# The down product of a Strassen-style MLP: another first half product, weights loaded at other steps, the last sums at another place

## The chip, the cores and the metric

The kernel runs on one NeuronCore of one Trainium2 chip. The metric is the device time of one execution, in microseconds (us). The kernel before takes 2855.52 us, the median of 3 runs (2850.24 to 2856.83). The engines are called by their names: TensorE (PE in the profile: matmuls; PEld its weight loads), VectorE (DVE), ScalarE (ACT), GpSimd (POOL) and SyncE (SP), which only issues transfers here. GpSimd issues transfers too, in order with its other work.

## The reference, cut to what matters

The program is one step of a two-layer encoder trunk for 1072 tokens (16 meta, 32 sample, 1024 prompt), width 1024. Each layer has a mixer and then an MLP, all in 32-bit floating point:

```python
def mlp(h, w_up, w_down):
    u = jax.nn.relu(h @ w_up)
    return (u * u) @ w_down
...
xp = xp + mlp(rmsnorm(xp, norm_mlp[l]), w_up[l], w_down[l])
xs = xs + mlp(rmsnorm(xs, norm_mlp[l]), w_up[l], w_down[l])
```

`w_up` is 1024 x 4096 and `w_down` 4096 x 1024. The change touches only the second product, `(u * u) @ w_down`, in both layers.

## The kernel before, in words

Every full-precision product is made of three matmuls of a high and a low part (`mm3`, lines 72 to 77): high by high, high by low, low by high. `hi_lo` (lines 62 to 68) makes the parts: ScalarE casts the high part (line 64), and VectorE (line 66) or GpSimd (line 68) subtracts it from the source to get the low part. The profile therefore shows nearly all such work under lines 64, 66 and 68, and the tiles tell what it is: `md_w` is a weight of the down product, `md_u` a pair of rows of its activations.

The MLP is done as seven half-size products in place of eight (Strassen's scheme in Winograd's form). **Up** runs over 16 blocks of 256 hidden units. For each, TensorE makes seven products; VectorE squares the results and subtracts them from each other, so that seven operands of the down product (B11, B21, B22, T1 to T4) lie in `xT`, and GpSimd's queue stores them to a buffer `ud` in memory, 1.9 MB per block (lines 987 to 1006). The store of the last block is kept back, and line 1088 issues it in the down product.

**Down** runs the seven products of `DOWN` (line 1010), each for two column halves c, so 14 half products, written (n, c) here. One has 16 steps kb. A step is 12 matmuls (four output blocks of three) with the weight `md_w{kb}` and one row of the activations; `acts` loads two rows at a time from `ud` into one of three buffers `md_ur` and splits them into one of four buffers `md_u`. During the half c = 1 of product n, `weights(n + 1, kb)` makes the weights of the next product as TensorE is done with the old ones (line 1122). The operands of the weights are quarters of `w_down`: A11, A12, A21, A22. Two are kept in `k1` and `k2`, four tiles of 1 MB each; the others come as `md_raw`, 256 KB each, in one of three buffers. A11 and A22 and A12 need no sums. S2 needs two on VectorE for each kb (A21 + A22, less A11: lines 1036 and 1037), S3 one (line 1041) and a copy on ScalarE, A22 one behind it (line 1055), S4 one (line 1047).

In the order before, A11 is the first product. Its quarter is loaded into `k1` in four transfers on SyncE's queue at the start, and A21 into `k2` in four on GpSimd's queue at steps 2, 6, 10 and 14 of (0,0). The low halves of the first three weights and of the first activations are made on GpSimd. S2 is the second product, so that its sums are made in (0,1).

The results are added to `xT` (line 1134), which holds the residual again: it was saved to memory (`xsave`) and is loaded back at step 4 of the products 0 to 3 (line 1116). A load on GpSimd's queue stands behind a copy of one element (`behind`, line 1068) that reads the current `md_u` and writes into the load's target; the load so waits for the cast of that pair.

What sets the order: TensorE runs in the order of the code. SyncE and GpSimd run in the order of the code up to (1,0), where `order.close()` stands; after that, and VectorE and ScalarE always, a scheduler sets the order by its own estimate of times when the program is built. Each engine then works through its queue in order.

Of the kernel before, what the change touches and what calls it, by code (L numbers as in the profile page):

```python
# [51 lines left out]
class Core:  # L52
# [879 lines left out]
    def up(self, sb, ps):  # L932
# [20 lines left out]
        for at, (b, n) in enumerate(todo):  # L953
# [39 lines left out]
            elif wn == "S3":  # L993
                squared(v["B22"], v["B22"])
            elif wn == "A22":
                tt(v["B21"], v["B21"], v["B21"], op=ALU.mult)
            elif wn == "S4":
                squared(v["B12"], v["B12"])
                for x, p, m in (("T1", "B12", "B11"), ("T2", "B22", "T1"), ("T3", "B22", "B12"), ("T4", "B21", "T2")):
                    tt(v[x], v[p], v[m], op=ALU.subtract)  # L1000
                store = partial(nc.gpsimd.dma_start, self.ud[b // 4][:, b % 4], place[:, b % 2, 1:8, :hw])
                if b < self.NP - 1:
                    store()
                else:
                    self.last_store = store
                del pairs[b]
# [3 lines left out]
    DOWN = (("A11", "B11", ("11",)), ("S2", "T2", ("12",)), ("S3", "T3", ("22",)), ("A22", "T4", ("21",)),  # L1010
            ("A12", "B21", ("11",)), ("S1", "T1", ("22", "12")), ("S4", "B22", ("12",)))


    def down(self, k1, k2, sb, ps, mid, done):
# [15 lines left out]
        def weights(n, kb, eng="v"):  # L1030
            x = self.DOWN[n][0]
            a, b = (k[kb // 4][:, kb % 4] for k in (k1, k2))
            if x == "A11":
                src = a
            elif x == "S2":
# [22 lines left out]
        def acts(n, c, g):  # L1058
# [4 lines left out]
            self.hi_lo(t, hl[:, 0], hl[:, 1], "g" if (n, c) == (0, 0) and g < 2 else "v")  # L1063
# [24 lines left out]
        self.last_store()  # L1088
        at = 0
        out = {}  # L1090
        for n, c in passes:
            x, _, to = self.DOWN[n]
            first = n in (0, 4, 5, 6)
# [4 lines left out]
            for kb in range(NP):  # L1098
# [18 lines left out]
                for ob in range(4):  # L1117
                    f = slice(P * ob, P * ob + P)
                    hl = w[n, kb]
                    self.mm3(out[c][ob], (hl[:, 0, f], hl[:, 1, f]), (u[:, 0, kb % 2], u[:, 1, kb % 2]), first and kb == 0, kb == NP - 1, n in (1, 2, 3))  # L1120
# [17 lines left out]
    def mlp(self, nms, mid, done):  # L1138
# [7 lines left out]
        with ExitStack() as st, tc.manual_schedule(engines={mybir.EngineType.PE}):  # L1146
# [14 lines left out]
            k2, k1 = ([kp.tile([P, 4, 512], F32, name=f"md_k{x}{y}") for y in range(4)] for x in (2, 1))  # L1161
# [679 lines left out]
```

## Time and profile before

| | before |
|---|---|
| median of 3 runs | 2855.52 us (2850.24 to 2856.83) |
| the profiled execution | 2860.78 us, span 2859.0 us |
| TensorE busy | 2642.7 us (92%) |
| VectorE busy | 1891.1 us (66%) |
| ScalarE busy | 1265.2 us (44%) |
| GpSimd busy | 631.0 us (22%) |
| down product of layer 0 | about 977 to 1328 us |
| down product of layer 1 | about 2490 to 2857 us |

Times in a row are microseconds from the start of the span. A row of the order of time gives the start, the duration, the engine, the line, the operation, out<-in with shapes and the count, and in brackets how long the engine sat idle before it and which engine's work ended that. A row by stretches gives the stretch, its length, each engine's busy time with its number of instructions (PE, PEld, DVE, ACT, POOL), the granted TensorE clock, the busy share of the transfer engines and GB/s. Matmuls are pipelined: how fast TensorE goes is read from the distance of the starts.

### The profile page before, as it was taken

The page shows a single profiled execution, that of the slowest core. Times are in us where ns is not written, and L with a number is a line of the kernel's source. Part 1 is how long each engine was busy: PE and PEld are TensorE (multiplying, and loading weights), DVE is VectorE, ACT ScalarE, POOL GpSimd, SP SyncE. Part 2 cuts the span into 40 slices and gives each one's busy share as a digit, 9 for nine tenths or more (in the row PEclk, how much of TensorE's full clock was granted, in tenths as well). Part 3 has the DMA queues.
Part 4 walks back from the last instruction along what each step waited for, and adds up shares of the span by engine and source line. Part 5 has one row for each costly group of instructions (what it writes and reads, how often), then busy time and mean ns, then how long its engine had stood idle before and what let it go on. Part 6 is the DMA issues. An engine that isn't in the chain of part 4 may idle for free. (4 is left out here: it accounts for less than half of the span.)

```text
span 2859.0 us, 49166 instructions
## 1 busy us (share of the span) xinstructions
PE 2642.7 (92%) x18377; PEld 2452.5 (86%) x18391; DVE 1891.1 (66%) x3846; ACT 1265.2 (44%) x2820; POOL 631.0 (22%) x693
## 2 busy tenths in 40 slices
PE   5899988878999999999999978999977999999998
PEld 5888966768999999999789856788767999989998
DVE  5934376687676677578643556778788676677553
ACT  4435454243333335445333346666653333435342
POOL 3423354200000210003110244555521000111000
PEclk9999988999999999999999979999988999999999
DMA  6343241132544577544465374344322434486643
GB/s 192 101 133 103 73 140 43 31 112 92 163 131 153 208 231 218 171 136 121 119 197 168 116 175 128 88 100 103 77 85 71 157 135 156 173 265 204 198 141 102
DMA packets 355926, 393.77 MB, mean 138 GB/s; under 512 B 41503, under 2 KB 292088, under 8 KB 353640
## 3 DMA queue, kind: packets, MB, share of 16 engines
q1 hardware_dynamic: 338728, 305.50, 37.6%
q0 software_dynamic: 16960, 85.13, 8.2%
q8 instruction: 145, 2.38, 0.4%
q14 instruction: 93, 0.76, 0.1%
HBM read 263.94 MB, written 125.48 MB: 136 GB/s over the span
## 5 line engine op out<-in xcount | busy, mean ns | idle before, releaser
L75 PE MATMUL bank<-pj_wh,h 128*128 128x384 f32 (+3 forms) x832 | 298.0, 360 | 9.5 <-ACT pj_wh L64 7.0
L77 PE MATMUL bank<-pj_wh,h 128*128 128x384 f32 (+3 forms) x832 | 296.1, 357 | 6.1 <-DVE h L66 4.8
L76 PE MATMUL bank<-pj_wl,h 128*128 128x384 f32 (+3 forms) x832 | 296.4, 357 | 3.4 <-DVE pj_wl L66 3.4
L76 PE MATMUL mu_y<-md_u,md_w 128*128 128x268 f32 (+1 forms) x896 | 260.6, 291 | 12.4 <-DVE md_u L66 10.4
L77 PE MATMUL mu_y<-md_u,md_w 128*128 128x268 f32 (+1 forms) x896 | 260.1, 290 | 6.1 <-POOL md_w L68 6.1
L75 PE MATMUL mu_y<-md_u,md_w 128*128 128x268 f32 (+1 forms) x896 | 261.3, 292 | 1.1 <-ACT md_u L64 1.0
L75 PE MATMUL bank<-md_u,md_w 128*128 128x268 f32 (+1 forms) x896 | 257.4, 287 | 0.1
L76 PE MATMUL bank<-md_u,md_w 128*128 128x268 f32 (+1 forms) x896 | 255.9, 286 | 1.5 <-DVE md_u L66 1.5
L77 PE MATMUL bank<-md_u,md_w 128*128 128x268 f32 (+1 forms) x896 | 255.5, 285 | 0.0
L64 ACT CAST md_u<-md_ur 128x536 fp32r<-128x536 f32 (+1 forms) x224 | 141.5, 636 | 230.4 <-PE mu_y L77 110.8
L66 DVE TENSOR_TENSOR md_u<-md_ur,md_u 128x536 fp32r<-128x536 f32 (+1 forms) x220 | 155.7, 711 | 129.9 <-ACT md_u L64 129.8
L76 PE MATMUL mu_y<-ho_T,mu_w 128*128 128x268 f32 (+1 forms) x768 | 219.2, 285 | 0.8 <-DVE ho_T L66 0.8
L77 PE MATMUL mu_y<-ho_T,mu_w 128*128 128x268 f32 (+1 forms) x768 | 219.3, 286 | 0.0
L75 PE MATMUL mu_y<-ho_T,mu_w 128*128 128x268 f32 (+1 forms) x768 | 218.5, 285 | 0.0
L1298 POOL TENSOR_TENSOR fx_p<-fx_p,sm_den 128x144 f32<-128x144 f32 (+7 forms) x128 | 150.6, 1177 | 181.8 <-DVE sm_den L1297 165.0
L66 DVE TENSOR_TENSOR mu_w<-mu_raw,mu_w 128x512 fp32r<-128x512 f32 x160 | 110.0, 688 | 116.3 <-ACT mu_w L64 116.3
L76 PEld LDWEIGHTS mu_y<-md_u,md_w 128*128 128x128 f32 x896 | 172.9, 193 | 14.5 <-DVE md_u L66 12.1
L64 ACT CAST mu_w<-mu_raw 128x512 fp32r<-128x512 f32 x160 | 99.2, 622 | 188.0 <-PE bank L77 124.6
L77 PEld LDWEIGHTS mu_y<-md_u,md_w 128*128 128x128 f32 x896 | 173.0, 193 | 6.5 <-POOL md_w L68 6.5
L75 PEld LDWEIGHTS bank<-pj_wh,h 128*128 128x128 f32 x832 | 158.8, 191 | 22.2 <-ACT pj_wh L64 7.5
L75 PEld LDWEIGHTS mu_y<-md_u,md_w 128*128 128x128 f32 x896 | 173.2, 193 | 1.8 <-ACT md_u L64 1.8
L77 PEld LDWEIGHTS bank<-pj_wh,h 128*128 128x128 f32 x832 | 158.4, 190 | 17.6 <-DVE h L66 5.1
(544 smaller groups left out, 8168.3 us busy)
## 6 DMA issues: line engine op xcount, KB each, us to landing
md_raw<-in_w_down SPq DMA_DIRECT2D x160, 256.0 KB
mu_raw<-in_w_up SPq DMA_DIRECT2D x64, 512.0 KB
ud<-xT POOLq DMA_DIRECT2D x16, 1876.0 KB, 7.5
md_ur<-ud SPq DMA_DIRECT2D x112, 268.0 KB
ud<-xT POOLq DMA_DIRECT2D x16, 1848.0 KB, 10.1
md_ur<-ud SPq DMA_DIRECT2D x112, 264.0 KB
fh_ka<-zk SPq DMA_DIRECT2D x32, 260.0 KB
md_k<-in_w_down SPq DMA_DIRECT2D x8, 1024.0 KB
```

What stands on the lines that cost most here:

```text
L64: nc.scalar.copy(hi, src)
L66: nc.vector.tensor_tensor(lo, src, hi.bitcast(F32), op=ALU.subtract)
L75: mm(out, ah, bh, start=start, stop=False)
L76: mm(out, ah, bl, start=False, stop=False)
L77: mm(out, al, bh, start=False, stop=stop)
L1298: nc.gpsimd.tensor_tensor(p[:, :n], p[:, :n], den[:, 0:1].to_broadcast([P, n]), op=ALU.mult)
```

## The change

The order of the seven products becomes A12, A11, S2, S3, A22, S1, S4. A12 is now the first and is loaded whole into `k2` at the start; nothing of it is needed later. A11 is loaded into `k1` in four transfers in (0,0) and (0,1), and A21 into `k2` in four in (1,0) and (1,1), all on GpSimd's queue, by a table `later` of steps. A12's 16 transfers of `md_raw` in each layer are gone. A12 and A11 add to the same quarter of the output and now both start new accumulators (`first`). The residual is loaded back at step 6 of the products 0, 2, 3 and 4.

GpSimd makes no low halves any more; VectorE makes them all. Four weights in place of six are made ahead of the first step. The squaring and the four sums of the last block, and its store, are put on a list, of which the down product takes one at each of its first six steps.

```diff
-                squared(v["B12"], v["B12"])
+                self.last = [partial(squared, v["B12"], v["B12"])]
                 for x, p, m in (("T1", "B12", "B11"), ("T2", "B22", "T1"), ("T3", "B22", "B12"), ("T4", "B21", "T2")):
-                    tt(v[x], v[p], v[m], op=ALU.subtract)
-                store = partial(nc.gpsimd.dma_start, self.ud[b // 4][:, b % 4], place[:, b % 2, 1:8, :hw])
-                if b < self.NP - 1:
-                    store()
-                else:
-                    self.last_store = store
+                    self.last.append(partial(tt, v[x], v[p], v[m], op=ALU.subtract))
+                self.last.append(partial(nc.gpsimd.dma_start, self.ud[b // 4][:, b % 4], place[:, b % 2, 1:8, :hw]))
+
+                while b < self.NP - 1 and self.last:
+                    self.last.pop(0)()
...
-    DOWN = (("A11", "B11", ("11",)), ("S2", "T2", ("12",)), ("S3", "T3", ("22",)), ("A22", "T4", ("21",)),
-            ("A12", "B21", ("11",)), ("S1", "T1", ("22", "12")), ("S4", "B22", ("12",)))
+    DOWN = (("A12", "B21", ("11",)), ("A11", "B11", ("11",)), ("S2", "T2", ("12",)), ("S3", "T3", ("22",)),
+            ("A22", "T4", ("21",)), ("S1", "T1", ("22", "12")), ("S4", "B22", ("12",)))
...
+            elif x == "A12":
+                src = b
...
-            self.hi_lo(t, hl[:, 0], hl[:, 1], "g" if (n, c) == (0, 0) and g < 2 else "v")
+            self.hi_lo(t, hl[:, 0], hl[:, 1])
...
-        load(k1[0], "A11", 0, 4)
+        load(k2[0], "A12", 0, 4)
         ready(0)
         for x in range(1, 4):
-            load(k1[x], "A11", 4 * x, 4)
-        for kb in range(6):
-            w[0, kb] = weights(0, kb, "g" if kb < 3 else "v")
-        self.last_store()
+            load(k2[x], "A12", 4 * x, 4)
+
+        later = {(0, 0, 10): (k1[0], "A11", 0), (0, 0, 14): (k1[1], "A11", 4), (0, 1, 2): (k1[2], "A11", 8), (0, 1, 6): (k1[3], "A11", 12),
+                 (1, 0, 4): (k2[0], "A21", 0), (1, 0, 8): (k2[1], "A21", 4), (1, 0, 12): (k2[2], "A21", 8), (1, 1, 0): (k2[3], "A21", 12)}
+        for kb in range(4):
+            w[0, kb] = weights(0, kb)
...
-            first = n in (0, 4, 5, 6)
+            first = n in (0, 1, 5, 6)
...
-                if n == 0 and c == 0 and kb + 6 < NP:
-                    w[0, kb + 6] = weights(0, kb + 6)
-                if n == 0 and c == 0 and kb % 4 == 2:
-                    x = k2[kb // 4]
+                if n == 0 and c == 0 and kb + 4 < NP:
+                    w[0, kb + 4] = weights(0, kb + 4)
+
+                if self.last:
+                    self.last.pop(0)()
+                if (n, c, kb) in later:
+                    x, name, k = later[n, c, kb]
                     behind(x[0:1, 0, 0:1], u)
-                    load(x, "A21", kb - 2, 4, nc.gpsimd)
-
-                if n < 4 and kb == 4:
+                    load(x, name, k, 4, nc.gpsimd)
+
+                if n in (0, 2, 3, 4) and kb == 6:
```

How the engines' queues change is seen in the built programs. Lines in rows of the changed program are its own: 1110 stands for the sums of 998 and 1000 that are now taken from the list, 1021 for the load of 1022, 1037 and 1038 for S2's sums of 1036 and 1037, 1069 and 1122 for 1068 and 1116, 1140 for the adds of 1134.

VectorE at the start of layer 0's down product, before; `md_w3` is the weight of step 3, `md_k10` the first tile of `k1`, and L985 the last work on a result of the up product:

```order
L985 TENSOR_TENSOR xT_3908<-xT_3908,bank_10059 128x268
L989 SCALAR_TENSOR_TENSOR xT_3908<-xT_3908 128x536
L1000 TENSOR_TENSOR xT_3908<-xT_3908 128x536 x4
L66 TENSOR_TENSOR md_w3_10237<-md_k10_10200,md_w3_10237 128x512
L66 TENSOR_TENSOR md_u_10221<-md_ur_10220,md_u_10221 128x536
L66 TENSOR_TENSOR md_w4_10240<-md_k11_10201,md_w4_10240 128x512
L66 TENSOR_TENSOR md_w5_10243<-md_k11_10201,md_w5_10243 128x512
```

And in the change:

```order
L985 TENSOR_TENSOR xT_3908<-xT_3908,bank_10059 128x268
L989 SCALAR_TENSOR_TENSOR xT_3908<-xT_3908 128x536
L1110 TENSOR_TENSOR xT_3908<-xT_3908 128x536 x4
L66 TENSOR_TENSOR md_w0_10223<-md_k20_10195,md_w0_10223 128x512
L66 TENSOR_TENSOR md_w1_10226<-md_k20_10195,md_w1_10226 128x512
L66 TENSOR_TENSOR md_w2_10229<-md_k20_10195,md_w2_10229 128x512
L66 TENSOR_TENSOR md_w3_10232<-md_k20_10195,md_w3_10232 128x512
L66 TENSOR_TENSOR md_u_10206<-md_ur_10205,md_u_10206 128x536
L66 TENSOR_TENSOR md_u_10211<-md_ur_10210,md_u_10211 128x536
L66 TENSOR_TENSOR md_u_10216<-md_ur_10215,md_u_10216 128x536
L66 TENSOR_TENSOR md_w4_10239<-md_k21_10196,md_w4_10239 128x512
```

In both programs the weights up to `md_w15` and then eight `md_u` follow. The squaring and the four sums stand together at their old place; the low halves of the first three weights and the first two pairs have moved here from GpSimd's queue.

VectorE where S2's sums begin; before, this is in (0,1), right behind the adds that close (0,0):

```order
L1134 TENSOR_TENSOR xT_3908<-xT_3908,mu_y_10250 128x268
L1036 TENSOR_TENSOR md_k20_10196<-md_k20_10196,md_raw_10547 128x512
L1036 TENSOR_TENSOR md_k20_10196<-md_k20_10196,md_raw_10566 128x512
L1037 TENSOR_TENSOR md_k20_10196<-md_k20_10196,md_k10_10200 128x512 x2
L66 TENSOR_TENSOR md_u_10574<-md_ur_10573,md_u_10574 128x536
L1036 TENSOR_TENSOR md_k20_10196<-md_k20_10196,md_raw_10590 128x512
L66 TENSOR_TENSOR md_w0_10551<-md_k20_10196,md_w0_10551 128x512
L66 TENSOR_TENSOR md_w1_10570<-md_k20_10196,md_w1_10570 128x512
```

In the change it is in (1,0), behind the adds that close (0,1) and the last weight of A11; `md_u_10884` is pair 4 of (1,0) and `md_u_10915` pair 5:

```order
L66 TENSOR_TENSOR md_w15_10813<-md_k13_10194,md_w15_10813 128x512
L66 TENSOR_TENSOR md_u_10855<-md_ur_10854,md_u_10855 128x536
L66 TENSOR_TENSOR md_u_10884<-md_ur_10883,md_u_10884 128x536
L1037 TENSOR_TENSOR md_k20_10195<-md_k20_10195,md_raw_11090 128x512
L1037 TENSOR_TENSOR md_k20_10195<-md_k20_10195,md_raw_11109 128x512
L1037 TENSOR_TENSOR md_k20_10195<-md_k20_10195,md_raw_11133 128x512
L1038 TENSOR_TENSOR md_k20_10195<-md_k20_10195,md_k10_10191 128x512 x2
L66 TENSOR_TENSOR md_u_10915<-md_ur_10914,md_u_10915 128x536
L1038 TENSOR_TENSOR md_k20_10195<-md_k20_10195,md_k10_10191 128x512
```

S2's sums have moved one product later, into a pass in which no weights are split. Nine of the 16 first sums and nine of the second stand ahead of the adds that close (1,0).

GpSimd behind the stores of the up product, in the change; before, five subtractions (line 68) and the last store stood here, and the four loads of A21 among the restores:

```order
L1110 DMA ud03_6543<-xT_3908 128x3752
L1069 COPY xT_3908<-md_u_10272 1x1 x2
L1122 DMA xT_3908<-xsave0_5904 128x2x268
L1069 COPY xT_3908<-md_u_10272 1x1 x2
L1122 DMA xT_3908<-xsave0_5904 128x2x268
L1069 COPY md_k10_10191<-md_u_10346 1x1
L1021 DMA md_k10_10191<-in_w_down 128x4x512
L1069 COPY md_k11_10192<-md_u_10422 1x1
L1021 DMA md_k11_10192<-in_w_down 128x4x512
```

The rest of A11's loads, the restore of (0,1) and the four loads of A21 follow.

More of the change, by code (lines that the diff above doesn't have):

```diff
@@ L1119, in down @@
                     hl = w[n, kb]
-                    self.mm3(out[c][ob], (hl[:, 0, f], hl[:, 1, f]), (u[:, 0, kb % 2], u[:, 1, kb % 2]), first and kb == 0, kb == NP - 1, n in (1, 2, 3))
+                    self.mm3(out[c][ob], (hl[:, 0, f], hl[:, 1, f]), (u[:, 0, kb % 2], u[:, 1, kb % 2]), first and kb == 0, kb == NP - 1, n in (2, 3, 4))
                 if c == 1 and n < 6:
@@ L1159, in mlp @@
             kp = pool(ks, "mk", "right")
-            k2, k1 = ([kp.tile([P, 4, 512], F32, name=f"md_k{x}{y}") for y in range(4)] for x in (2, 1))
+            k1, k2 = ([kp.tile([P, 4, 512], F32, name=f"md_k{x}{y}") for y in range(4)] for x in (1, 2))
             sb = pool(st, "md")
```

## The prediction

> **What bounds the kernel now.** I read the page's busy shares first, then TensorE's order of time through both down products, cut it into the fourteen half products by the switch of its output between `mu_y` and `bank`, and asked for busy times by these stretches.
>
> ```profile
> PE 2642.7 (92%) x18377; PEld 2452.5 (86%) x18391; DVE 1891.1 (66%) x3846; ACT 1265.2 (44%) x2820; POOL 631.0 (22%) x693
> ...
> 977.39:1012.18 34.79, 28.05 (x194) 26.86 (x193) 22.56 (x28) 12.58 (x23) 17.74 (x21) 0.90 0.79 271
> 1012.18:1037.17 24.99, 24.33 (x194) 23.90 (x193) 22.61 (x40) 9.57 (x16) 2.21 (x6) 1.00 0.77 253
> 1037.17:1064.87 27.70, 24.32 (x194) 23.90 (x193) 22.70 (x40) 9.89 (x17) 4.35 (x12) 1.00 0.67 186
> 1064.87:1088.67 23.80, 23.80 (x194) 23.80 (x193) 17.13 (x28) 16.34 (x28) 1.51 (x5) 1.00 0.65 195
> 1088.67:1112.47 23.80, 23.80 (x194) 23.80 (x193) 17.09 (x30) 11.85 (x20) 3.42 (x8) 1.00 0.68 205
> ...
> 2489.84:2523.10 33.26, 27.22 (x195) 26.23 (x193) 21.65 (x27) 11.93 (x22) 17.93 (x20) 0.90 0.80 283
> 2523.10:2548.13 25.03, 24.15 (x194) 23.53 (x193) 23.27 (x41) 9.83 (x17) 2.88 (x6) 1.00 0.79 261
> 2548.13:2576.99 28.86, 25.39 (x194) 24.97 (x193) 22.64 (x41) 9.90 (x17) 3.98 (x12) 0.94 0.61 177
> 2576.99:2600.35 23.36, 23.36 (x194) 23.36 (x193) 16.68 (x27) 15.97 (x28) 1.04 (x3) 1.00 0.65 195
> ```
>
> TensorE is the bound: undisturbed, a half product takes 23.80 us in layer 0 and 23.36 in layer 1 (0.124 and 0.122 us per matmul, 1.49 per step of 12). Only the first three are longer. Call them (n, c), n the product and c the column half. Layer 0 loses 10.99, 1.19 and 3.90 us in (0,0), (0,1) and (1,0); layer 1 loses 9.90, 1.67 and 5.50. These 33.2 us are all that this change can reach directly. The next rows say what they are.
>
> ```profile
> 979.09 0.39 PE L76 MATMUL mu_y<-md_u,md_w 128*128 128x268 f32 x1 [1.01 <-POOL md_u L68]
> 982.53 0.59 PE L77 MATMUL mu_y<-md_u,md_w 128*128 128x268 f32 x1 [3.06 <-POOL md_w L68]
> 982.92 0.43 PE L75 MATMUL mu_y<-md_u,md_w 128*128 128x268 f32 x1
> ...
> 988.50 0.33 PE L76 MATMUL mu_y<-md_u,md_w 128*128 128x268 f32 x1
> ...
> 995.62 0.39 PE L76 MATMUL mu_y<-md_u,md_w 128*128 128x268 f32 x1 [1.33 <-DVE md_u L66]
> ...
> 1005.52 0.39 PE L75 MATMUL mu_y<-md_u,md_w 128*128 128x268 f32 x1 [0.84 <-ACT md_u L64]
> 1006.27 0.39 PE L76 MATMUL mu_y<-md_u,md_w 128*128 128x268 f32 x1 [0.36 <-DVE md_u L66]
> ...
> 1039.06 0.39 PE L76 MATMUL mu_y<-md_u,md_w 128*128 128x268 f32 x1 [1.60 <-DVE md_u L66]
> 1044.07 0.40 PE L76 MATMUL mu_y<-md_u,md_w 128*128 128x268 f32 x1 [1.78 <-DVE md_u L66]
> ...
> 2555.06 0.43 PE L76 MATMUL mu_y<-md_u,md_w 128*128 128x264 f32 x1 [1.81 <-DVE md_u L66]
> ...
> 2558.59 0.33 PE L77 MATMUL mu_y<-md_u,md_w 128*128 128x264 f32 x1
> ```
>
> In (0,0), TensorE waits for the low halves that GpSimd makes until 982.53, then issues at half rate (982.92 to 988.50 is 25 matmuls, 0.223 apart: 25 x 0.099 = 2.5 us lost), then waits twice more for activations, about 3.3 us with the slow restarts. In (0,1) and (1,0) it waits for low halves of activations on VectorE, which is busy 22.6 of 24.99 us: there the sums for S2 stand in VectorE's queue ahead of the activations. Layer 1 has one more slow stretch there, 2555.06 to 2558.59, 3.5 us at half rate and some 1.5 us lost.
>
> **The start.** Rows of VectorE and GpSimd there, and three that give spacings:
>
> ```profile
> 958.58 1.97 DVE L1000 TENSOR_TENSOR xT<-xT 128x536 f32<-128x536 f32 x3
> ...
> 978.06 1.54 DVE L989 SCALAR_TENSOR_TENSOR xT<-xT 128x536 f32<-128x536 f32 x1
> 979.64 6.85 DVE L1000 TENSOR_TENSOR xT<-xT 128x536 f32<-128x536 f32 x4
> ...
> 987.01 0.70 DVE L66 TENSOR_TENSOR md_u<-md_ur,md_u 128x536 fp32r<-128x536 f32 x1
> 987.64 7.30 DVE L66 TENSOR_TENSOR md_w<-md_k,md_w 128x512 fp32r<-128x512 f32 x12
> ...
> 1012.44 1.46 DVE L1134 TENSOR_TENSOR xT<-xT,mu_y 128x268 f32<-128x268 f32 x4
> ...
> 1035.28 0.69 DVE L66 TENSOR_TENSOR md_w<-md_k,md_w 128x512 fp32r<-128x512 f32 x1
> 1035.88 0.69 DVE L1037 TENSOR_TENSOR md_k<-md_k,md_k 128x512 f32<-128x512 f32 x1
> ...
> 977.71 3.06 POOL L68 TENSOR_TENSOR md_u<-md_ur,md_u 128x536 fp32r<-128x536 f32 x2 [14.56 <-ACT md_u L64]
> 980.74 5.17 POOL L68 TENSOR_TENSOR md_w<-md_k,md_w 128x512 fp32r<-128x512 f32 x3
> 986.78 0.56 POOL L1088 DMA_DIRECT2D ud<-xT  x1 [0.87 <-DVE xT L1000]
> ```
>
> The same sums take 0.65 us each (1.97 / 3) at 958.58 and 1.71 (6.85 / 4) while GpSimd subtracts beside them. The Trainium skill (SBUF — State Buffer, Who interferes with whom) says that a VectorE instruction with two inputs in SBUF and a GpSimd instruction that reads SBUF hold one port in turn, each blocking the other; the trace agrees, 1.71 against 0.65. By the rule the sums fall back to 0.65 once GpSimd has nothing to subtract; if the 1.71 had another cause, the start would be 5.3 us later, the second rival below.
>
> The change takes these five instructions from GpSimd and gives them to VectorE. The diff spreads the last sums over steps, but VectorE is not in the hand-written order, and in its new queue all five stand together ahead of the low halves. So the second matmul waits for ten instructions: five sums at 0.65 (first spaced 0.64), four `md_w` at 0.61 (7.30 / 12) and one `md_u` of 0.70: 978.06 + 3.25 + 2.43 + 0.70 = 984.4, where TensorE now resumes at 982.5. That is 1.9 us worse: idle about 7.0 instead of 5.1. The half-rate stretch should stay: 2.5.
>
> What follows gets better. Pair 3 of the activations comes after two more `md_u` (1.26) and the twelve `md_w`: 984.4 + 1.26 + 7.3 + 0.7 = 993.7; TensorE wants it after six steps, 984.4 + 25 x 0.223 + 47 x 0.124 = 995.8. Its buffer is freed at 984.4 and the load has till 992. Pair 6 takes pair 3's buffer.
>
> ```profile
> 995.60 0.36 SPq L1062 DMA_DIRECT2D md_ur<-ud  x1
> ...
> 1004.83 0.64 ACT L64 CAST md_u<-md_ur 128x536 fp32r<-128x536 f32 x1 [5.22 <-DMA md_ur<-ud]
> ...
> L1068 POOL COPY md_k<-md_u x4: 193/570/726, 987.3 to 1006.4; 1x1 f32<-1x1 f32 x4
> L1022 POOL DMA_DIRECT2D md_k<-in_w_down x4: 748/750/794, 988.0 to 1007.5; - x4
> ...
> DMA to landing us min/median/max: 8.4/9.4/11.5
> ```
>
> Now that load takes 9.2 us (995.60 to 1004.83) amid the last store (issued late, at 986.8) and two 1 MB loads. In the change the store goes at about 981.4, and the four loads of a resident half leave for later steps. Even with 9.2: 993.7 + 9.2 + 0.64 + 0.70 = 1004.3, wanted at 995.8 + 6 x 1.49 = 1004.7. So the 3.3 us of later waits go: (0,0) loses 7.0 + 2.5 = 9.5 in place of 10.99. In layer 1, scaled by 23.36 / 23.80, 9.3 replaces 9.90. **Together 2.1 us gained.** If the later waits stay, 1.9 a layer is lost, 3.8; if the half rate is as short as the 1.5 us of the stretch at 2555, each layer gains 1.0 more. So -3.8 to +4.1.
>
> A rule bears on the 2.5. The Trainium skill (TensorE: Matmul & The Clock Gate, Part 1) says that the clock drops to half after an idle window of about 3.4 us and returns after a busy one, the windows running free. By it a restart costs half of 3.4 to 6.8 us, an estimate of 1.7 to 3.4; the trace's 5.6 us lie inside. By the rule the sum would move by -0.8 to +0.9 a layer. By it waits of under 2 us would also leave (1,0) of layer 1 at full rate; the trace differs, the granted clock there is 0.94.
>
> **Sums for S2.** Before, all 32 sums (lines 1036, 1037, spaced 0.60 like the low halves: 1035.28 to 1035.88) fall into (0,1) and its tail, since S2 is the second product. VectorE's work in that pass: 32 x 0.60 + 16 `md_w` x 0.60 + 8 `md_u` x 0.63 + 4 adds x 0.36 = 35.3 us against 23.8. In the change the second product is A11, which needs only low halves: 9.6 + 5.0 + 1.4 = 16 us in (0,1). S2's sums get (1,0) and (1,1): 9 of 16 rows' sums stand ahead of the adds that close (1,0), the rest among the low halves of (1,1). That pass then holds 14 sums, 16 `md_w`, 8 `md_u`, 4 adds and 3 sums of S3: 26.3 us, of which six `md_w` run over. S3's pass, with 16 sums, 16 `md_w`, 8 `md_u` and 4 adds, asks 25.7 us now and runs in 23.80 without a wait. So 12.26 us (1.19 + 3.90 + 1.67 + 5.50) can go.
>
> What is late next are the loads of A21, moved from GpSimd's queue at steps 2 to 14 of (0,0) to steps of (1,0). Behind each stands, on VectorE, a sum that needs it, and behind that the low half of a pair. The first load's copy waits for the cast of pair 2 of (1,0), which stands behind the cast of weight 13, released at step 14 of (0,1), 3.0 us before its end; two casts (0.62 and 0.64), the copy (up to 0.73) and the issue (0.75) use most of these, and I leave it none. It lands 9.4 us into (1,0); five sums (3.0) and pair 5 (0.7) end at 13.1; TensorE wants pair 5 at step 10, 14.9. Spare: 1.8. At the longest landing, 11.5, it is 0.3 late. The next loads have 3 us or more. A11's loads are issued some 6 steps, 8.9 us, ahead and block only a cast of weights. I charge 0.6 us a layer: **11 us gained**, between 12.3 and nothing.
>
> **The rest.** 32 `md_raw` issues on SyncE become 8 loads on GpSimd, the same bytes; SyncE has room. The scheduler reorders some matmuls and VectorE work of layer 1's input product; the waits there are small.
>
> ```profile
> PE bank L75 <- DVE pc_z L278: 2.3, 1, 2.3
> PE bank L75 <- ACT pj_wh L64: 1.9, 1, 1.9
> ```
>
> I take 0, between +4 and -4. **Sum:** 2.1 + 11 = 13.1. The profiled execution took 2860.78 (span 2859.0 and 1.8 around it): 2847.7. The median of the runs, 2855.52, lies 5.3 below the profiled one, so 2842.4: I predict **2843 us**.
>
> **Rivals.** *The overload only moves* (0.22). For it: the sums are as many, with three `md_raw` buffers, and VectorE stays in order. Against: S3's pass. If half of the 11 us returns, 2848.5; if all, 2854. *The sums stay slow* (0.05): if the 1.71 us is not GpSimd's doing, the start is 5 x 1.06 = 5.3 us later in each layer, 2853.6. Against: the row at 958.58. *Slower: A21 lands late* (0.11). The first load of A21 stands in GpSimd's in-order queue behind restores and copies. Each us of landing beyond 11.2 stops VectorE with pair 5 behind it, and TensorE; a stop of that size also costs a 2.5 us restart. All is lost from (13.1 / 2 - 2.5) = 4.1 us beyond, a landing of 15.3. At 19 us, twice the median: 7.8 + 2.5 = 10.3 a layer, 2863.6. For: nine GpSimd loads in a row. Against: no load of this kind took over 11.5 while engines and queues were busier.
>
> **How the numbers follow.** The forecast has 0.62; its own range is 2837 to 2849 (better: the restarts' 2.0 and the input product's 4; worse: 3 a layer in waits left over). About 0.2% is what a measurement here can tell, 2849.8 to 2861.2. Faster: 0.62 and the milder part of the first rival, 0.68; same: the rest of it and the second, 0.22; slower 0.10. The range, 2835 to 2857, takes in the first two rivals and leaves out the slow one.
>
> **What would show it.** In the changed profile: the five sums in 3.3 us, the second matmul waiting for `md_u` on VectorE until about 7 us after the last up matmul, then half rate for 3 to 6 us; no waits later in (0,0); (0,1), (1,0) and (1,1) at 23.8 and 23.4. Wrong, if (1,0) or (1,1) wait for `md_u` behind line 1037 of the new text, or if the rows wait for `md_k`.

## The result and the profile after

The changed kernel took 2840.12 us, the median of 4 runs (2839.52 to 2840.55), beside 2856.18 us (2850.24 to 2862.49) for the kernel before: a ratio of 0.9942, 95% interval 0.9928 to 0.9957. In a second comparison it took 2843.70 us (5 runs) beside 2856.55 (11 runs), 0.9960 (0.9948 to 0.9972). So it is 13 to 16 us faster. The prediction said 2843, that is 12.5 us less than the median known then.

The changed kernel's page, then the busy times by half products (stretch, length, busy time of PE, PEld, DVE, ACT and POOL with their counts, granted clock, share of the transfer engines, GB/s):

```profile
PE 2636.6 (93%) x18391; PEld 2446.6 (86%) x18391; DVE 1886.5 (66%) x3856; ACT 1264.3 (45%) x2820; POOL 628.1 (22%) x699
```
```profile
970.55:1002.84 32.29, 25.61 (x194) 25.25 (x193) 21.12 (x35) 12.69 (x23) 10.67 (x13) 0.89 0.83 285
1002.84:1026.64 23.80, 23.80 (x194) 23.80 (x193) 16.67 (x28) 13.76 (x23) 5.09 (x10) 1.00 0.62 197
1026.64:1050.44 23.80, 23.80 (x194) 23.80 (x193) 17.68 (x31) 5.66 (x9) 4.17 (x6) 1.00 0.95 326
1050.44:1074.24 23.80, 23.80 (x194) 23.80 (x193) 23.05 (x40) 13.78 (x25) 0.93 (x1) 1.00 0.62 192
2478.17:2510.48 32.31, 25.69 (x195) 25.33 (x193) 20.97 (x35) 12.66 (x23) 10.80 (x13) 0.89 0.85 288
2510.48:2533.84 23.36, 23.36 (x195) 23.36 (x193) 16.54 (x28) 13.70 (x23) 4.15 (x10) 1.00 0.61 204
2533.84:2557.20 23.36, 23.36 (x195) 23.36 (x194) 17.07 (x30) 5.61 (x9) 4.54 (x7) 1.00 0.95 329
```

The loss of a half product is its length less 23.80 us in layer 0 and 23.36 in layer 1; the first one is counted from the moment at which the next matmul would have started behind the last of the up product (970.55 here, 977.39 before). (0,0) now loses 8.49 and 8.95 us, where it lost 10.99 and 9.90. (0,1) and (1,0) lose nothing, where they lost 12.26 in the two layers together. That is 15.7 us given back in the half products that the edit reaches.

TensorE's order of time shows what is left of the start:

```profile
970.84 0.39 PE L75 MATMUL mu_y<-md_u,md_w 128*128 128x268 f32 x1
977.78 0.59 PE L76 MATMUL mu_y<-md_u,md_w 128*128 128x268 f32 x1 [6.55 <-DVE md_u L66]
978.17 0.43 PE L77 MATMUL mu_y<-md_u,md_w 128*128 128x268 f32 x1
...
980.80 0.28 PE L77 MATMUL mu_y<-md_u,md_w 128*128 128x268 f32 x1
```

One wait, for VectorE's low half of `md_u`, and then 12 matmuls at half rate (978.17 to 980.80, 0.219 apart). VectorE and GpSimd in the same stretch:

```profile
971.22 0.72 DVE L989 SCALAR_TENSOR_TENSOR xT<-xT 128x536 f32<-128x536 f32 x1
971.97 2.72 DVE L1110 TENSOR_TENSOR xT<-xT 128x536 f32<-128x536 f32 x4
974.61 2.49 DVE L66 TENSOR_TENSOR md_w<-md_k,md_w 128x512 fp32r<-128x512 f32 x4
977.01 1.96 DVE L66 TENSOR_TENSOR md_u<-md_ur,md_u 128x536 fp32r<-128x536 f32 x3
```
```profile
975.22 0.53 POOL L1110 DMA_DIRECT2D ud<-xT  x1 [18.91 <-ACT md_w L64]
```

The reader sees the ten instructions that the prediction counted, one behind the other: the five last sums, which the code spreads over steps, stand together ahead of the low halves. The four sums take 2.72 us, 0.68 each, where they took 6.85 beside GpSimd's subtractions.

The two profiles differ by more, 2859.0 less 2838.4 = 20.6 us. The rest shows no tie to the change: the down product of layer 0 starts 6.8 us sooner in this profile, though the engines' work up to shortly ahead of it has the same order, 2.8 us are lost again on the way to layer 1, and (6,0) of layer 1 loses 7.8 us in place of 8.9. Profiles of several kernels with that same order put the first matmul of the down product of layer 0 anywhere from 965.97 to 978.69 us (the same kernel twice: 970.84 and 968.57), and (6,0) of layer 1 loses 7.0 to 8.6 us in the other kernels. So the half products, which repeat within about 2 us, are the better measure of an edit, and the medians confirm them.

### The profile page after: what moved, and what is told of

Read it like the earlier page. It is cut to its first block, busy times and chain, and to the rows that moved or that the text cites. A ratio compares the mean times of both kernels' runs of the same rounds, so it can differ in the third digit from the quotient of the medians.

```text
span 2838.4 us, 49134 instructions
## 1 busy us (share of the span) xinstructions
PE 2636.6 (93%) x18391; PEld 2446.6 (86%) x18391; DVE 1886.5 (66%) x3856; ACT 1264.3 (45%) x2820; POOL 628.1 (22%) x699
## 4 chain that ended last, share of the span: by engine, by line
PE 72%; DVE 7%; DMA 2%; ACT 2%; issue 1%; POOL 0%; SPq 0%; DVEq 0%; ACTq 0%
PE bank L75 12%; PE bank L76 11%; PE bank L77 11%; PE mu_y L76 8%; PE mu_y L77 8%; PE mu_y L75 8%; PE bank L1491 3%; PE bank L1501 2%; PE bank L1502 1%; PE fx_s L1473 1%; PE fx_s L1474 1%; DMA md_raw<-in_w_down 1%; PE bank L257 1%; DVE xT L873 1%; PE bank L1198 1%
## 5 line engine op out<-in xcount | busy, mean ns | idle before, releaser
L76 PEld LDWEIGHTS mu_y<-md_u,md_w 128*128 128x128 f32 x896 | 171.3, 191 | 13.6 <-DVE md_u L66 13.4
L76 PEld LDWEIGHTS bank<-pj_wl,h 128*128 128x128 f32 x832 | 159.7, 192 | 16.1 <-DVE pj_wl L66 4.7
L75 PEld LDWEIGHTS mu_y<-md_u,md_w 128*128 128x128 f32 x896 | 171.2, 191 | 0.8 <-ACT md_u L64 0.7
```

Of the source, the lines that this page charges most:

```text
L75: mm(out, ah, bh, start=start, stop=False)
L76: mm(out, ah, bl, start=False, stop=False)
```

## The experiments

Losses in us by half product, layer 0 / layer 1, all counted as above from TensorE's starts (the first ones contain the 0.29 and 0.34 us of delay ahead of the first matmul). The last two columns are medians; "before" is the kernel before, run beside it. The half products behind (1,1) are not in the table; where one loses over 2 us more than it does before, the text says so.

| kernel | (0,0) | (0,1) | (1,0) | (1,1) | median | before |
|---|---|---|---|---|---|---|
| before | 10.99 / 9.90 | 1.19 / 1.67 | 3.90 / 5.50 | 0 / 0 | | |
| changed, first profile | 8.49 / 8.95 | 0 / 0 | 0 / 0 | 0 / 0 | 2840.12 | 2856.18 |
| changed, again | 9.34 / 8.95 | 0 / 0 | 0 / 0 | 0 / 0 | 2843.70 | 2856.55 |
| order alone | 10.99 / 10.94 | 0 / 0.37 | 0.60 / 0.43 | 1.28 / 2.20 | 2849.81 | 2855.30 |
| low halves alone | 9.67 / 12.53 | 0.49 / 0 | 3.91 / 3.84 | 0 / 0 | 2850.43 | 2855.30 |
| low halves back on GpSimd | 9.29 / 9.42 | 0 / 0 | 0 / 0 | 0 / 0 | 2844.86 | 2855.30 |
| VectorE in written order | 8.07 / 11.98 | 1.32 / 0 | 0 / 0 | 0.29 / 0 | 2846.66 | 2855.30 |
| and the store in two | 4.55 / 4.53 | 0 / 0 | 0 / 0 | 2.01 / 0 | 2838.75 | 2856.55 |
| and the low halves first | 4.00 / 4.87 | 0 / 0 | 0 / 0 | 1.25 / 0 | 2835.63 | 2856.55 |
| the same again | 3.74 / 5.89 | 0 / 0 | 0 / 0 | 0.66 / 2.19 | 2832.91 | 2856.15 |
| four buffers for the loads | 3.12 / 2.83 | 0 / 0 | 0 / 0 | 0 / 0 | 2861.92 | 2856.15 |
| A21 eight steps later | 8.93 / 8.53 | 0 / 0 | 0 / 0 | 0 / 0 | 2843.41 | 2856.55 |

### The changed kernel again

> The changed kernel again, with more runs beside the kernel before and beside the kernels of this call. Theory (what the half products lose is fixed by the program, 8.2 and 8.6 us in (0,0), nothing in the next three; the spread of the runs lies in what comes ahead of the down product, which starts anywhere from 966 to 978 us in profiles of the same program): the half products repeat within 0.3 us, and the medians differ by 16.3 us, the sum of what the passes gave back, within 3: 13 to 19 less than before. Rival (the first comparison, four runs on a side, was partly luck): less than 12 us.

Measured: 12.9 us less than before, a ratio of 0.9960 (0.9948 to 0.9972). (0,0) loses 9.34 and 8.95 us, the others nothing. 15.7 and 14.9 us are given back in the half products of the two profiles, 16.1 and 12.9 in the medians. 12.9 lies just under the 13 to 19 that were expected and above the rival's 12. The expected repetition within 0.3 us was missed in one place: (0,0) of layer 0 lost 0.85 us more, and all of that is the stretch at half rate, 20 matmuls in place of 12 behind the same wait (6.93 and 6.94 us).

### The order alone

```diff
-    DOWN = (("A11", ...), ("S2", ...), ("S3", ...), ("A22", ...), ("A12", ...), ("S1", ...), ("S4", ...))
+    DOWN = (("A11", ...), ("A12", ...), ("S2", ...), ("S3", ...), ("A22", ...), ("S1", ...), ("S4", ...))
```

> The kernel before with one thing changed: its products run A11, A12, S2, S3, A22, S1, S4, A12 second and read piece by piece into `md_raw`, so that the sums for S2 fall behind an A12 pass that needs only low halves. The low halves of the start stay on GpSimd, the last sums and the store stay where they were, and A21 is still loaded into its resident tiles in (0,0). Theory (the 12.26 us of (0,1) and (1,0) were VectorE's 32 sums for S2 standing ahead of the activations' low halves): (0,1), (1,0) and (1,1) at 23.8 and 23.36 us with no waits, (0,0) still losing 9.9 to 11 us a layer; 12.3 us less than before, about 2844 us. Rival (those waits came with the store and the loads of the start and would only move): (1,0) or (1,1) waits in place of (0,1), and the whole stays within 4 us of before, 2852 to 2856.

In this kernel S2, S3 and A22 accumulate onto A12's product in place of A11's, so that it computes something else with the same instructions. Measured: 2849.81 us, 5.5 less than before, 0.9976 (0.9965 to 0.9988). Of the 12.26 us of (0,1) and (1,0), 10.9 are gone (0 + 0.37 + 0.60 + 0.43 = 1.40 are left), but 1.28 and 2.20 come anew in (1,1). There VectorE has almost no gap, 24.94 us busy of 25.08:

```profile
1008.29:1032.09 23.80, 23.80 (x195) 23.80 (x193) 14.11 (x23) 10.87 (x19) 2.54 (x6) 1.00 0.80 255
1032.09:1056.49 24.40, 24.06 (x194) 23.85 (x193) 21.25 (x36) 8.42 (x14) 0.00 (x0) 1.00 0.88 271
1056.49:1081.57 25.08, 24.35 (x195) 23.92 (x193) 24.94 (x44) 13.84 (x27) 16.26 (x1) 1.00 0.61 172
```

So both are half right. The order is what frees (0,1), and it alone gives back 12.26 - 4.88 = 7.4 us of the 12.26; the rest moves to (1,1), as the rival *the overload only moves* has it. In the changed kernel (1,1) runs without a wait, with VectorE 23.05 us busy of 23.80. A full VectorE is not enough to explain the waits: in the run with A21 eight steps later it is busy for all of (1,1) of layer 0 (its row stands below), and nothing waits there. The two kernels differ in VectorE's order, in where A12 comes from and in when A21 is loaded; which of these makes the 4.9 us was not taken apart.

### The low halves alone

```diff
-            self.hi_lo(t, hl[:, 0], hl[:, 1], "g" if (n, c) == (0, 0) and g < 2 else "v")
+            self.hi_lo(t, hl[:, 0], hl[:, 1])
...
-            w[0, kb] = weights(0, kb, "g" if kb < 3 else "v")
+            w[0, kb] = weights(0, kb)
```

> The kernel before with one thing changed: the five low halves of the start (two of `md_u`, three of `md_w`) go from GpSimd to VectorE, the order of products and all loads as before. Theory (GpSimd's subtractions made VectorE's last sums slow, and the later waits of (0,0) followed from these late sums and low halves): the five sums take 3.3 us in place of 8.4, the second matmul resumes 7 us after the last up matmul, no waits of more than 0.3 us later in (0,0), which loses 8.2 to 9.5 us a layer in place of 9.9 to 11; (0,1) and (1,0) lose their 12.26 as before; 2 to 4 us less than before, 2852 to 2854. Rival (the later waits of (0,0) come from the four loads of A21 that share the DMA engines with the activations' loads): sums fast, but waits for `md_u` of 2 to 3.5 us a layer stay, (0,0) loses 11 to 13 us, and the time is 0 to 6 us above before, 2856 to 2862.

Measured: 2850.43 us, 0.9989 (0.9976 to 1.0001), which can't be told from before for certain and lies below what either theory expected. The sums are fast, 2.72 us for four, and the second matmul waits 6.93 us as in the changed kernel. But the rival is right in layer 1: TensorE still waits at step 6 for pair 3, 1.95 and 0.74 us with a new stretch at half rate behind, and (0,0) loses 12.53. In layer 0 the load of that pair comes just in time; its cast stands idle for 9.62 us until it lands:

```profile
982.86 0.64 ACT L64 CAST md_u<-md_ur 128x536 fp32r<-128x536 f32 x1 [9.62 <-DMA md_ur<-ud]
```

In the changed kernel the same cast, at 983.10, sat idle for 4.99 us. In (0,0) the low halves on VectorE alone gain 1.3 us in one layer and lose 2.6 in the other. In the changed kernel, where A21's loads have left (0,0) as well, both layers lose less. That (0,1) and (1,0) lose 8.2 us in place of 12.26 was expected by neither theory; behind the later end of (0,0) in layer 1 the waits of (0,1) are gone, and that is as far as the trace tells it.

### The low halves back on GpSimd

The reverse edit, made to the changed kernel.

> The changed kernel with one thing undone: the five low halves of the start go back to GpSimd (`md_u` of the first two pairs, `md_w` 0 to 2); order of products and spread loads stay as changed. Theory (port shared by GpSimd's subtractions and VectorE's sums, and A21's loads out of (0,0) remove the later waits): the four subtractions take 1.7 us each again, the second matmul resumes 5 to 5.6 us after the last up matmul, 1.5 to 2 us sooner than in the changed kernel, and (0,0) loses 6.5 to 8 us a layer if nothing waits later: 2836 to 2840. Rival (the later waits of (0,0) came from the slow sums and the late store): they come back, 2 to 3.5 us a layer, (0,0) loses 9 to 11 us, 2842 to 2846. (0,1) to (1,1) at full speed in both.

Measured: 2844.86 us, 0.9968 (0.9957 to 0.9979), within the rival's range. The sums are slow again, and the restart is indeed sooner, but TensorE then waits for pair 3, whose low half stands behind twelve `md_w` that all start late:

```profile
976.09 1.55 DVE L989 SCALAR_TENSOR_TENSOR xT<-xT 128x536 f32<-128x536 f32 x1
977.68 6.86 DVE L1110 TENSOR_TENSOR xT<-xT 128x536 f32<-128x536 f32 x4
984.46 0.68 DVE L66 TENSOR_TENSOR md_w<-md_k,md_w 128x512 fp32r<-128x512 f32 x1
985.07 0.70 DVE L66 TENSOR_TENSOR md_u<-md_ur,md_u 128x536 fp32r<-128x536 f32 x1
985.69 7.30 DVE L66 TENSOR_TENSOR md_w<-md_k,md_w 128x512 fp32r<-128x512 f32 x12
992.92 1.33 DVE L66 TENSOR_TENSOR md_u<-md_ur,md_u 128x536 fp32r<-128x536 f32 x2
```
```profile
977.12 0.39 PE L76 MATMUL mu_y<-md_u,md_w 128*128 128x268 f32 x1 [1.01 <-POOL md_u L68]
980.58 0.59 PE L77 MATMUL mu_y<-md_u,md_w 128*128 128x268 f32 x1 [3.06 <-POOL md_w L68]
...
993.68 0.39 PE L76 MATMUL mu_y<-md_u,md_w 128*128 128x268 f32 x1 [1.86 <-DVE md_u L66]
```

Four sums take about 6.86 us whenever GpSimd subtracts beside them (this kernel, the one with the order alone, the kernel before) and 2.72 whenever it doesn't (the changed kernel and the one with the low halves alone). The Trainium skill (SBUF — State Buffer, Who interferes with whom) says that a VectorE instruction with two inputs in SBUF contends with a GpSimd instruction that reads SBUF, and the traces agree. The price of the slow sums in time is small, though: (0,0) loses 9.29 and 9.42 us in place of 8.49 to 9.34 and 8.95, about 0.9 us in the two layers together.

### VectorE in the written order

```diff
-        order.enter_context(self.tc.manual_schedule(engines={mybir.EngineType.SP, mybir.EngineType.Pool}))
+        order.enter_context(self.tc.manual_schedule(engines={mybir.EngineType.SP, mybir.EngineType.Pool, mybir.EngineType.DVE}))
```

> The changed kernel with VectorE put under the hand-written order too, from the start of the down product to the end of the second product's predecessor ((0,0) and (0,1)), so that the last sums really go one per step, behind the first low halves. Theory (the wait before the second matmul is nothing but the count of VectorE instructions ahead of it): the wait falls from ten instructions to one for the second matmul and four for the third, 6.9 us to about 3 together; (0,0) loses 3 to 6 us a layer in place of 8.2 and 8.6; 2830 to 2835 us. Rival (the store, now about 4 us later, makes the last pairs of activations late): waits for `md_u` of pairs 6 and 7 near the end of (0,0), 2 to 4 us a layer, and 2836 to 2842 us.

Measured: 2846.66 us, 0.9971 (0.9962 to 0.9981), not better than the changed kernel and above both expected ranges. Both theories hold, each at its place. The start is as short as the count says, waits of 1.02 and 1.86 us in place of 6.94. But the last sum is now made at 986.30, the store leaves behind it, and pair 7, which it feeds, is loaded late. TensorE's rows (the last one is of layer 1), then VectorE's, GpSimd's and ScalarE's:

```profile
975.15 0.39 PE L76 MATMUL mu_y<-md_u,md_w 128*128 128x268 f32 x1 [0.63 <-DVE md_u L66]
977.01 0.39 PE L77 MATMUL mu_y<-md_u,md_w 128*128 128x268 f32 x1 [1.47 <-DVE md_w L66]
...
1001.54 0.39 PE L75 MATMUL mu_y<-md_u,md_w 128*128 128x268 f32 x1 [2.17 <-ACT md_u L64]
...
2514.79 0.59 PE L75 MATMUL mu_y<-md_u,md_w 128*128 128x264 f32 x1 [4.29 <-ACT md_u L64]
```
```profile
986.30 0.70 DVE L1110 TENSOR_TENSOR xT<-xT 128x536 f32<-128x536 f32 x1
```
```profile
987.53 0.53 POOL L1110 DMA_DIRECT2D ud<-xT  x1 [27.94 <-issue]
```
```profile
1000.85 0.64 ACT L64 CAST md_u<-md_ur 128x536 fp32r<-128x536 f32 x1 [12.69 <-DMA md_ur<-ud]
```

In layer 1 the same wait is twice as long and 17 matmuls at half rate follow it; so (0,0) loses 11.98 us there, more than in the changed kernel.

### The store in two

```diff
+                if b == self.NP - 1:
+                    nc.gpsimd.dma_start(self.ud[b // 4][:, b % 4, 0:3], place[:, b % 2, 1:4, :hw])
+                f = 3 if b == self.NP - 1 else 0
-                self.last.append(partial(nc.gpsimd.dma_start, self.ud[b // 4][:, b % 4], place[:, b % 2, 1:8, :hw]))
+                self.last.append(partial(nc.gpsimd.dma_start, self.ud[b // 4][:, b % 4, f:7], place[:, b % 2, 1 + f:8, :hw]))
```

> The kernel with VectorE in the written order (last sums one per step, behind the first low halves), with one more thing: the store of the last block is cut in two, the three parts that are ready before the last sums (B11, B21, B22) at once, the four sums T1 to T4 behind them. Theory (the wait at step 14 there, 2.2 us in layer 0 and 4.3 in layer 1, is the store that left 12 us later, at 987.5, with pair 7 behind it): this wait goes, (0,0) loses only its first two waits, 2.6 to 3 us a layer, with no half-rate stretch; 10 to 12 us less than the changed kernel. Rival (pair 7 is late because its load waits for a buffer or shares the DMA engines with the loads of A11): the wait stays at 2 to 4 us a layer, 2 to 6 us above or below the changed kernel.

Measured: 2838.75 us beside 2843.70 for the changed kernel, 0.9941 (0.9929 to 0.9953) of before: 5 us less than the changed kernel, where 10 to 12 were expected. The wait at step 14 is gone: A12's operand B21 needs none of the last sums, and its store now leaves ahead of the last up matmul (971.03). GpSimd's row:

```profile
969.83 0.53 POOL L1002 DMA_DIRECT2D ud<-xT  x1 [12.92 <-DVE xT L996]
```

(0,0) loses 4.55 and 4.53 us. The first two waits are as expected; the stretch at half rate that was thought to go stayed, 15 and 16 matmuls. New waits for `md_u` in layer 0, of 0.70 and 1.28 us in (1,1) and others in (4,0), cost 2.01 and 2.17 us; where they come from is not shown.

### The low halves first

```diff
+                    add = partial(tt, u["B12"], u["B12"], out, op=ALU.add)
+                    if b < self.NP - 1:
+                        add()
+                    else:
+                        adds.append(add)
...
         load(k2[0], "A12", 0, 4)
+        for kb in range(4):
+            w[0, kb] = weights(0, kb)
         ready(0)
```

> As the kernel with the store in two, and the two adds that close the last block of the up product (line 985) are deferred too, so that VectorE makes the low halves of `md_w` 0 to 3 while the last up matmuls run, then `md_u`. Theory (the restart is the count of VectorE instructions between the last up matmul and the low half of `md_u` 0 and `md_w` 0): only the cast of `md_u` 0 and its low half are left, 0.6 to 1.2 us of waiting, (0,0) loses 0.6 to 1.5 us a layer, 2 to 4 us less than the kernel with the store in two, 13 to 15 less than the changed kernel. Rival (the deferred work lands on VectorE in (0,0) and holds back a low half later): waits of 1 to 3 us at steps 4 to 8, no better than the kernel with the store in two.

> The kernel with the low halves first again, beside the kernel with four buffers and the kernel before. Theory (the passes are fixed by the program): (0,0) loses 3.7 and 4.5 us within 0.5, and the time is 18 to 24 us below the kernel before. Rival (its lead over the changed kernel, 8 us from five runs, was partly luck): 14 to 17 us below the kernel before, no better than the changed one.

Measured: 2835.63 us (0.9928, 0.9916 to 0.9939, of before), and 2832.91 us when it ran again (0.9918, 0.9900 to 0.9937). It beats both kernels, by 20.9 to 23.2 us the one before and by 8.1 the changed one beside which it ran. The wait before the second matmul is down to 1.18 us, and no stretch at half rate follows it. What is left of (0,0) is pair 3's load at step 6, which makes three matmuls late, 2.6 and 3.3 us from start to start in all in the first profile. SyncE issues it from 975.81 on, and the cast that waits for it starts at 985.15 (the first row is the busy times of (0,0), the second ScalarE's):

```profile
974.37:1002.17 27.80, 25.31 (x195) 24.20 (x193) 18.92 (x34) 12.89 (x23) 10.66 (x13) 1.00 0.82 277
```
```profile
985.15 0.64 ACT L64 CAST md_u<-md_ur 128x536 fp32r<-128x536 f32 x1 [0.48 <-DMA md_ur<-ud]
```

The expected loss of (0,0), 0.6 to 1.5 us, was too low by that wait, and the lead over the changed kernel is 8.1 us in place of 13 to 15; the rival's place, step 6, was right but its cause, VectorE's load, was not: VectorE sat idle there, until the cast.

The second profile of this kernel keeps the time that was expected of it, 18 to 24 us below before, but not the half products: in layer 1 (0,0) loses 5.89 us, because behind the same three late matmuls 16 run at half rate this time, and (1,1) loses 2.19.

### Four buffers for the loads

```diff
-            t = sb.tile([P, 2, QMAX], F32, name="md_ur", bufs=3)[:, :, :qw]
+            t = sb.tile([P, 2, QMAX], F32, name="md_ur", bufs=4)[:, :, :qw]
...
-            t = sb.tile([P, 512], F32, name="md_raw", bufs=3)
+            t = sb.tile([P, 512], F32, name="md_raw", bufs=2)
```

> As the kernel with the low halves first, with four `md_ur` buffers in place of three, so that the activations' pair 3 is loaded ahead of the start, and, for the room, two `md_raw` buffers in place of three. Theory (the waits that are left there, 2.6 us in layer 0 and 3.3 in layer 1 at step 6, are pair 3's load, issued only when the cast of pair 0 freed its buffer and 9.3 us under way): these waits go, (0,0) loses 1.0 to 2 us a layer, 4 to 6 us less than that kernel, 2829 to 2832 us. Rival (two `md_raw` buffers hold back the sums, which use one piece each): waits for `md_u` or `md_w` of 1 to 4 us a layer in (1,0) to (2,1) or in the later products, and no gain or 2 to 6 us of loss, 2835 to 2842 us.

Measured: 2861.92 us, slower than before, 1.0016 (1.0005 to 1.0026), and 29 us above the kernel with the low halves first beside which it ran, far dearer than the rival had it. (0,0) does lose less, 3.12 and 2.83 us. But the weights of S3 come late: the half product (3,0) loses 9.76 and 9.04 us. TensorE waits for `md_w` there, and VectorE, which makes its low half, for the pieces of `w_down` that have now two buffers:

```profile
1136.59 0.40 PE L77 MATMUL mu_y<-md_u,md_w 128*128 128x268 f32 x1 [1.85 <-DVE md_w L66]
1142.12 0.59 PE L75 MATMUL mu_y<-md_u,md_w 128*128 128x268 f32 x1 [2.53 <-ACT md_w L64]
```
```profile
1135.24 0.69 DVE L1049 TENSOR_TENSOR md_k<-md_k,md_raw 128x512 f32<-128x512 f32 x1 [2.37 <-DMA md_raw<-in_w_down]
```
```profile
PE mu_y L145 <- DVE nm_acc L139: 9.0, 1, 9.0
```

A wait of 9.0 us for the norm that follows the down product comes as well, in (6,1) of layer 0 (the last row, from the waits of TensorE behind 1200 us); the changed kernel has none there. Together that is 9.76 + 9.04 + 9.0 = 27.8 us. Against it stand 6.5 us that (0,0) and (1,1) lose less than in the second profile of the low halves first, so that about 21 of the 29 us are accounted for. The two buffer counts were not changed one at a time, so that the two buffers are the cause is argued from the rows.

### A21 eight steps later

```diff
-                 (1, 0, 4): (k2[0], "A21", 0), (1, 0, 8): (k2[1], "A21", 4), (1, 0, 12): (k2[2], "A21", 8), (1, 1, 0): (k2[3], "A21", 12)}
+                 (1, 0, 12): (k2[0], "A21", 0), (1, 1, 0): (k2[1], "A21", 4), (1, 1, 4): (k2[2], "A21", 8), (1, 1, 8): (k2[3], "A21", 12)}
```

> The changed kernel with the four loads of A21 eight steps (12 us) later, at steps (1,0,12), (1,1,0), (1,1,4) and (1,1,8). It asks for the price of a late A21, the slower rival of the prediction. In the changed kernel the first load landed 5.4 us into (1,0) and the low half behind its first five sums was done 5.8 us ahead of its use. Theory (the sums for S2 have room until their weights are used in (2,0), and VectorE's order is made anew for the later loads): the sums run over into the end of (1,1) and the start of (2,0), waits of 0 to 3 us a layer, 0 to 6 us above the changed kernel. Rival (a late load stops VectorE with the activations behind it): waits of 4 to 10 us a layer, at half rate behind them, 8 to 20 us above the changed kernel, slower than before at the upper end.

Measured: 2843.41 us beside 2843.70 for the changed kernel: no price that the runs show, and no wait in (1,0), (1,1) or (2,0). The first sum that needs A21 starts 18.3 us into (1,0) (1053.24, the pass starts at 1034.93), where it started 5.4 us into it in the changed kernel (1032.04, the pass starts at 1026.64). VectorE's row and the busy times of (1,1) here, and then three rows of the changed kernel:

```profile
1053.24 1.90 DVE L1037 TENSOR_TENSOR md_k<-md_k,md_raw 128x512 f32<-128x512 f32 x3 [1.84 <-DMA md_k<-in_w_down]
```
```profile
1058.73:1082.53 23.80, 23.80 (x194) 23.80 (x193) 23.80 (x41) 12.47 (x23) 3.42 (x4) 1.00 0.89 286
```
```profile
1032.04 1.90 DVE L1037 TENSOR_TENSOR md_k<-md_k,md_raw 128x512 f32<-128x512 f32 x3 [0.83 <-DMA md_k<-in_w_down]
1033.85 1.28 DVE L1038 TENSOR_TENSOR md_k<-md_k,md_k 128x512 f32<-128x512 f32 x2
1035.06 0.71 DVE L66 TENSOR_TENSOR md_u<-md_ur,md_u 128x536 fp32r<-128x536 f32 x1
```

The scheduler put the sums behind the activations of all of (1,0) when it knew of the later loads, so the sums no longer stand ahead of them. What this does not show is a load that comes late against the order it was planned for, because moving the loads changed the plan too.

## Why the prediction was right, step by step

**The time.** 2843 was forecast as the likeliest, within 2837 to 2849; measured were 2840.12 and 2843.70. By its own terms 13.1 us were to be gained in the half products, and 15.7 and 14.9 were. Both terms were put somewhat low, for the reasons below; that the second median lies within 1 us of 2843 is partly luck, since the two medians of this kernel are 3.6 us apart. One reading was too narrow: in layer 1 the first three half products are not the only long ones. The last five lose 1.3 to 8.9 us in the kernel before, where transposes of the result (line 1618) stand between the matmuls, and in (6,0) TensorE waits 3.4 us for the last adds besides. They are much the same in the changed kernel, so the sum does not suffer.

**The sums for S2** (11 us forecast, 12.26 measured). (0,1) needs 16.67 us of VectorE (16 was the estimate) and nothing waits. (1,1) holds 23.05 us, about the estimate of 26.3 less the six low halves that were to run over. The charge of 0.6 us a layer for A21 was not due: the first sum on A21 ran 5.4 us into (1,0), not 9.4, because the load was issued 1.0 us ahead of the pass, at 1025.64, and the sum could start 6.4 us later (1032.04), where 0 and 9.4 were assumed; the low half behind it ended at 1035.77, 5.7 us ahead of its use at step 10 (1026.64 + 14.88 = 1041.5), where 1.8 was forecast. The slower rival did not come: A21's loads landed within 5.7 to 8.8 us in the two profiles, where 15.3 would have cost the gain. Whether its 0.11 was too much no run shows, since the run with A21 eight steps later had VectorE's order made anew.

**The start** (2.1 us forecast, 3.45 and 2.6 measured). The count of instructions was right: the second matmul runs 7.23 us behind (977.78 less 970.55), and 7.0 was forecast. No wait comes later in (0,0), as forecast. The term that was mis-sized is the stretch at half rate, put at 2.5 us a layer: 8.49 - 7.23 = 1.3 and, in layer 1, 8.95 - 7.17 = 1.8 (2.1 and 1.8 in the second profile). The reason for the later waits was only half named. Fast sums alone don't remove them, as the run with the low halves alone shows (12.53 us in layer 1); and with the loads moved but the sums slow, in the run with the low halves back on GpSimd, the wait at step 6 stays. The prediction had both, but not that neither is enough.

**The rivals.** *The sums stay slow* fell: 0.68 us each without GpSimd, 1.71 with it, in five kernels. *The overload only moves* was not seen in the changed kernel, but it was in the run with the order alone, which keeps 4.9 of the 12.26 us, 3.5 of them newly in (1,1). This suggests, and does not show, that the outcome was nearer to this rival than the forecast's 0.62 had it.

**The rest** was put at 0 within 4 us. The way from the one down product to the other took 2478.50 - 970.84 = 1507.7 us in one profile of the changed kernel and 2481.57 - 968.57 = 1513.0 in the other, so such a difference is the run's and not the change's:

```profile
970.84 0.39 PE L75 MATMUL mu_y<-md_u,md_w 128*128 128x268 f32 x1
...
2478.50 0.39 PE L75 MATMUL mu_y<-md_u,md_w 128*128 128x264 f32 x1 [0.17 <-ACT md_u L64]
```
```profile
968.57 0.39 PE L75 MATMUL mu_y<-md_u,md_w 128*128 128x268 f32 x1
...
2481.57 0.39 PE L75 MATMUL mu_y<-md_u,md_w 128*128 128x264 f32 x1 [0.17 <-ACT md_u L64]
```

## What to carry to other kernels

Work whose result is needed late should not stand in an in-order queue ahead of work that the bound engine waits for; but what the late work feeds, here a store and through it a load, moves with it and has to be cut loose first. Read the order that was built and not the order that was written: the code here spread five sums over steps, and they stood together, because their engine was not under the written order. Where profiles with the same work ahead of a stage start it up to 13 us apart, compare the lengths of the stages that the edit touches, and let the medians confirm the sum.

## What the runs showed of the hardware

The number of slow matmuls does not go by the length of the wait. Behind one wait of 6.8 to 6.9 us, eight restarts in four profiled runs (the changed kernel twice, low halves alone, A21 later) had 12 to 21 matmuls at half rate, 2.6 to 4.7 us. Waits of about 1.0 and 1.85 us, one matmul apart (VectorE in order, the store in two), were followed by 15 or 16 such matmuls, 3.5 us, in four of four restarts. A single wait of 1.18 us was followed by none in six of six. The granted clock (the third figure from the end of a row) says why the counts differ. The rows are of the changed kernel, of its second profile and of the kernel with VectorE in order:

```profile
973.89:980.72 6.83, 2.94 (x13) 2.94 (x14) 6.79 (x13) 4.22 (x9) 0.53 (x1) 0.50 0.87 322
```
```profile
973.51:980.34 6.83, 4.83 (x21) 4.84 (x22) 6.83 (x13) 2.32 (x5) 0.00 (x0) 0.50 0.93 331
```
```profile
977.37:980.78 3.41, 3.41 (x18) 3.41 (x17) 3.41 (x7) 3.41 (x7) 0.00 (x0) 0.50 0.91 317
```

The clock is at 0.50 for 6.83 us behind the long wait and for 3.41 behind the two short ones; in these four half products of all twelve profiles it is never low for any other length. What differs is the moment: in the two profiles of the changed kernel it falls 3.05 and 4.94 us behind the first matmul (970.84 and 968.57), so that 12 matmuls in one and 20 in the other are left for the slow clock. The Trainium skill (TensorE: Matmul & The Clock Gate, Part 1) tells of an idle window of about 3.4 us before the clock drops and a busy one of about that length before it returns, both running free. The traces agree with the length and with the windows running free; but the drop behind waits of 2.9 us together does not need an idle stretch of 3.4.

GpSimd's work beside a busy VectorE can last long too. In the run with the order alone one of its adds took 17.68 us in (1,1), where VectorE had almost no gap; the same add took 0.93 us in the changed kernel. That it waited for VectorE is not taken apart.

```profile
1065.31 17.68 POOL L136 TENSOR_TENSOR nm_acc<-nm_acc,nm_t 128x268 f32<-128x268 f32 x1 [53.89 <-ACT nm_t L134]
```
